# Hybrid attention block in fp32: the `p @ w_ple` tiles at the first norm, the second norm by halves of 256 tokens

## The chip, the cores and the metric

The kernel runs on one core of a Trainium2 chip. The metric is the device time of one execution in microseconds (us); lower is better. The kernel before was run three times.

## The reference

One transformer block over 512 tokens of width 1024, all in fp32. The output must be this, for one layer:

```python
h = rmsnorm(x, attn_pre_g)
proj = h @ w_in                      # split into the q, k, v of both attentions and gates
mix = concatenate([o_nsa, o_swa], -1) @ w_o
x = x + rmsnorm(mix, attn_post_g)    # the first norm of this text
h = rmsnorm(x, mlp_pre_g)
gu = h @ w_gate_up                   # 1024 x 5632
a, u = split(gu, [2816], -1)
a = causal_dwconv(a, conv_w, conv_b) # three taps along the tokens
y = (gelu(a) * u) @ w_down           # 2816 x 1024
x = x + rmsnorm(y, mlp_post_g)       # the second norm
e = p @ w_ple                        # 256 x 1024
x = x + e * sigmoid(x @ w_ple_gate)  # 1024 x 1024
```

`o_nsa` is an attention of eight heads over compressed, selected and windowed keys, `o_swa` one of eight heads over a window of 128 tokens with sinks. The change does not touch them.

## The kernel before

Activations lie transposed: channels on the 128 partitions, the 512 tokens along the free axis, so that a width of 1024 is eight tiles of 128x512. Every product of two fp32 matrices is made of three fp32r matmuls (`mm3`, line 130): the high part of the weight by the high part of the activation (L134), the low part of the weight by the high part (L137), the high part of the weight by the low part of the activation (L138). `weight` (L113) brings a weight tile in: SyncE issues its load into one of two raw buffers (`wr`, L127), ScalarE copies the high part out (L118), VectorE subtracts it for the low part (L122). The raw buffer is free for the next load when the subtraction is done.

The program is written phase by phase, and a scheduler that works on a simulated timeline sets the order of each engine's instructions; only where `keep_in_program_order` is called does the written order stand. On the chip each engine runs its list in that order and waits on semaphores.

- **Out-projection.** `out_proj` (L787) makes eight tiles. The first half of each, over the first four tiles of the attention's mix, is made earlier between attention work (`fill` in the names) and kept in `mo`. `out_proj` makes the second half by 12 matmuls (`mixmm`, L769 to L771) into one of two PSUM buffers `mm`, and VectorE adds it to `mo` (L802). ScalarE squares the sum (L219, L222), and GpSimd or, at the last tile, VectorE adds up the squares (L223). The last tile of the mix is written by ScalarE (L519) and GpSimd (L520) after VectorE's L517.
- **First norm.** `norm_add` (L811) wants the reciprocal root mean square of 512 tokens. `rstd_col` (L190) sums over partitions by small matmuls with ones (L194); VectorE (L198) and GpSimd (a power, L200) make the root. `rstd_row` (L203) brings it back to a row by four transposes (L207). Then, for each of eight tiles `c`, VectorE scales (L829) and adds to the residual (L830), ScalarE writes the high part of `h` (L834; L832 at the second norm), VectorE its low part one step later (L843; L841).
- **`p @ w_ple`.** Beside each norm stand four of the eight tiles of `p @ w_ple` (`ple_tile`, L859, six matmuls and a copy out of PSUM by ScalarE, L864): two before the column sums, one before the row, one after. Their operands are loaded and split by `ple_load` (L847), once for each half, at the last tile of the out-projection and of the down-projection.
- **Gate/up and down.** `chunkwise` (L884) makes the first four gate/up tiles together, chunk by chunk of the inner dimension, so that each `h` tile is used four times (12 matmuls) as it appears. Then `mlp_up` (L892) makes the others tile by tile, 24 matmuls each. `mlp_down` (L916) makes eight tiles of 66 matmuls.
- **Second norm and gate.** `norm_add` again, then `ple_gate` (L938): four tiles by `chunkwise`, four one by one, with sigmoid, product, sum and output.

All matmuls of these phases are 512 tokens wide. The pool of large tiles `u` has 23 slots, `wh` six (three weights).

## Time and profile before

| | |
|---|---|
| median of three runs | 686.6 us (685.11 to 687.87) |
| the profiled execution | 687.33 us |
| its span, first to last instruction | 685.4 us |
| mean granted TensorE clock | 0.992 |
| matmuls (PE) | 666.0 us busy, 97% |
| VectorE (DVE) | 400.1 us busy, 58% |
| ScalarE (ACT) | 325.2 us busy, 47% |
| GpSimd (POOL) | 170.8 us busy, 25% |
| DMA queue of the loads (q1) | 32.6% of 16 engines' span |

The profile comes from one execution. An instruction's row names its engine, its source line and its tiles, output first; `mlpup_pss` is a tile of the phase `mlpup` in the PSUM buffer `s`. The idle time of an engine before a row stands in brackets with what ended it. The row of a matmul is longer than the distance to the next one, since matmuls are pipelined. The clock is given as a share of its full rate: 1.00 is 2.4 GHz and 0.50 is 1.2 GHz.

### The profile page before, as it was taken

Reading aid. Unit: us, or ns where it says so; the run is one execution under the profiler, and the core shown is the slowest. Engines: PE = TensorE matmul, PEld = TensorE weight load, DVE = VectorE, ACT = ScalarE, POOL = GpSimd, SP = SyncE. Lnnn points to the kernel's source line nnn. Section 1 sums busy time; section 2 is a strip of 40 time slices with the busy share of each in tenths; the row PEclk is TensorE's granted clock in tenths of the full one; section 3 lists DMA queues with packets and bytes.
Section 4 is the critical chain, followed back from the end, with each engine's and each line's share of the span. In section 5 each row is a group of like instructions: output and inputs, shape, how many; then the busy total and the mean of one; then the engine's idle time right before and its main releaser. Section 6 shows DMA issues by size and latency. Waiting matters only on the chain.

```text
span 685.4 us, 8840 instructions
## 1 busy us (share of the span) xinstructions
PE 666.0 (97%) x3111; PEld 546.6 (80%) x3111; DVE 400.1 (58%) x808; ACT 325.2 (47%) x603; POOL 170.8 (25%) x235
## 2 busy tenths in 40 slices
PE   8999999999998998999999999999999999999996
PEld 7988767777786876888888888888888888887785
DVE  6785777877846569577555555455542232235853
ACT  7553778876867564354334333333432222233341
POOL 1112677755646244321111010111100000100000
PEclk9999999999998999999999999999999999999999
DMA  8547523101143252133322223332323323344032
GB/s 292 165 112 219 153 62 77 47 2 47 47 127 120 77 193 69 53 102 95 120 94 92 93 92 97 107 105 93 92 85 96 96 85 114 90 141 154 1 107 77
DMA packets 25115, 70.05 MB, mean 102 GB/s; under 512 B 3184, under 2 KB 4464, under 8 KB 25072
## 3 DMA queue, kind: packets, MB, share of 16 engines
q1 hardware_dynamic: 24928, 69.42, 32.6%
q8 instruction: 24, 0.39, 0.2%
q14 instruction: 19, 0.16, 0.1%
q10 hardware_dynamic: 144, 0.08, 0.0%
HBM read 60.05 MB, written 2.10 MB: 91 GB/s over the span
## 4 chain that ended last, share of the span: by engine, by line
PE 86%; DVE 5%; ACT 3%; DMA 2%; POOL 1%; issue 1%; SPq 0%; ACTq 0%; POOLq 0%; DVEq 0%
PE mlpup_pss L138 5%; PE mlpup_pss L137 5%; PE mlpup_pss L134 4%; PE mlpup_psmm L137 3%; PE mlpup_psmm L134 3%; PE mlpup_psmm L138 3%; PE nsa_pso L534 3%; PE mlpup_pst L138 3%; PE mlpup_pst L134 3%; PE mlpup_pst L137 3%; PE mlpdown_pss L134 2%; PE mlpdown_pss L138 2%; PE mlpdown_pss L137 2%; PE nsa_pst L501 2%; PE mlpdown_pst L138 1%; PE mlpdown_psmm L138 1%
## 5 line engine op out<-in xcount | busy, mean ns | idle before, releaser
L118 ACT ACTIVATE mlpup_wh<-mlpup_wr 128x1024 fp32r<-128x1024 f32 x40 | 42.3, 1061 | 84.5 <-PE mlpup_pss L137 28.9
L877 POOL TENSOR_TENSOR mlpup_s<-mlpup_s,r3b 128x512 f32<-128x512 f32 x22 | 29.2, 1331 | 188.0 <-ACT mlpup_s L876 188.0
L118 ACT ACTIVATE mlpdown_wh<-mlpdown_wr 128x1024 fp32r<-128x1024 f32 (+1 forms) x24 | 23.7, 989 | 84.7 <-PE mlpdown_pss L137 33.9
L122 DVE TENSOR_TENSOR mlpdown_wh<-mlpdown_wr,mlpdown_wh 128x1024 fp32r<-128x1024 f32 (+1 forms) x24 | 27.3, 1135 | 62.2 <-ACT mlpdown_wh L118 62.2
L122 DVE TENSOR_TENSOR mlpup_wh<-mlpup_wr,mlpup_wh 128x1024 fp32r<-128x1024 f32 x40 | 49.4, 1236 | 11.8 <-ACT mlpup_wh L118 11.7
L137 PE MATMUL mlpup_pss<-r_u,mlpup_wh 128*128 128x512 f32 x120 | 46.8, 390 | 0.2 <-DVE mlpup_wh L122 0.2
L134 PE MATMUL mlpup_pss<-r_u,mlpup_wh 128*128 128x512 f32 x120 | 46.8, 390 | 0.0
L138 PE MATMUL mlpup_pss<-r_u,mlpup_wh 128*128 128x512 f32 x120 | 46.7, 389 | 0.0
L523 POOL TENSOR_SCALAR nsa_u<-nsa_u,nsa_nrc,gate 128x512 f32<-128x512 f32 (+3 forms) x64 | 38.5, 617 | 22.2 <-DVE nsa_nrc L652 16.6
L621 ACT ACTIVATE nsa_u<-nsa_u,nsa_nnm 128x512 f32<-128x512 f32 (+3 forms) x64 | 35.4, 554 | 5.3 <-DVE nsa_nnm L617 5.1
L505 DVE TENSOR_TENSOR nsa_u<-nsa_pst,nsa_u 128x512 fp32r<-128x512 f32 (+1 forms) x43 | 29.0, 684 | 9.1 <-ACT nsa_u L503 8.8
L122 POOL TENSOR_TENSOR fill_wh<-fill_wr,fill_wh 128x512 fp32r<-128x512 f32 (+1 forms) x14 | 24.7, 1767 | 33.9 <-ACT fill_wh L118 33.9
L617 DVE CUSTOM_DVE_ANT_0 nsa_u<-nsa_pss,biastables_u 128x512 f32<-128x512 f32 (+3 forms) x64 | 29.9, 486 | 5.3 <-PE nsa_pss L555 4.9
L223 POOL TENSOR_TENSOR mlpdown_s<-mlpdown_s,mlpdown_s 128x512 f32<-128x512 f32 x6 | 7.8, 1295 | 100.2 <-ACT mlpdown_s L222 100.2
L876 ACT ACTIVATE mlpup_s<-mlpup_s 128x512 f32<-128x512 f32 x22 | 13.8, 631 | 38.6 <-DVE mlpup_s L875 38.6
L503 ACT ACTIVATE nsa_u<-nsa_pst 128x512 fp32r<-128x512 f32 (+1 forms) x43 | 25.1, 592 | 13.4 <-PE nsa_pst L501 13.1
L134 PE MATMUL mlpup_pst<-r_u,mlpup_wh 128*128 128x512 f32 x80 | 31.2, 390 | 0.0
L138 PE MATMUL mlpup_pst<-r_u,mlpup_wh 128*128 128x512 f32 x80 | 31.1, 389 | 0.0
L137 PE MATMUL mlpup_pst<-r_u,mlpup_wh 128*128 128x512 f32 x80 | 31.1, 389 | 0.0
L134 PE MATMUL mlpup_psmm<-r_u,mlpup_wh 128*128 128x512 f32 x80 | 31.1, 389 | 0.0
L137 PE MATMUL mlpup_psmm<-r_u,mlpup_wh 128*128 128x512 f32 x80 | 31.1, 389 | 0.0
L138 PE MATMUL mlpup_psmm<-r_u,mlpup_wh 128*128 128x512 f32 x80 | 31.1, 389 | 0.0
(386 smaller groups left out, 1937.9 us busy)
## 6 DMA issues: line engine op xcount, KB each, us to landing
mlpup_wr<-in_gu_dram SPq DMA_DIRECT2D x40, 512.0 KB, 3.3
mlpdown_wr<-in_down_dram SPq DMA_DIRECT2D x16, 512.0 KB, 3.5
fill_wr<-in_win_dram SPq DMA_DIRECT2D x6, 512.0 KB, 3.8
mlpdown_wr<-in_down_dram SPq DMA_DIRECT2D x8, 384.0 KB, 3.2
fill_u<-fill_u SPq DMA_DIRECT2D x20, 128.0 KB, 2.8
loadx_u<-in_xT_dram SPq DMA_DIRECT2D x8, 256.0 KB, 5.0
compress_u<-projk_u SPq DMA_DIRECT2D x16, 128.0 KB, 2.4
fill_wr<-in_wo_dram SPq DMA_DIRECT2D x8, 256.0 KB, 3.1
```

The source lines that it names most:

```text
L118: nc.scalar.activation(hi, raw, AF.Copy)
L122: eng.tensor_sub(lw, raw, hi.bitcast(F32))
L134: r = self.pin(mm(ps, hi, x[:, 0, :], start=start, stop=False))
L137: mm(ps, lo, x[:, 0, :], start=False, stop=False)
L138: mm(ps, hi, x[:, 1, :], start=False, stop=stop)
L503: nc.scalar.activation(t[:rows, 0, :], pt[:rows], AF.Copy)
L505: nc.vector.tensor_sub(lo, pt[:rows], t[:rows, 0, :].bitcast(F32))
L523: self.nc.gpsimd.tensor_scalar(ap, ap, col, gate, op0=ALU.mult, op1=ALU.mult)
L534: self.att(nc.tensor.matmul(po, v, rhs, start=start, stop=stop))
L617: nc.vector.tensor_tensor_reduce(dst, src, dist, op0=ALU.add, op1=ALU.min, scale=SLOPES[8 + 4 * g + r], scalar=3e38, accum_out=nm[:, r, b ...
L621: nc.scalar.activation(dst, dst, AF.Exp, bias=nm[:, r, b : b + 1], scale=-1.0, accum_out=sm[:, r, b : b + 1])
L877: nc.gpsimd.tensor_mul(c0, c0, self.r3)
```

## The change

Four things are done.

1. `ple_load` is called once, at the third tile of the out-projection, and loads both halves of `w_ple`; all eight `p @ w_ple` tiles stand at the first norm, four before the column sums, two before the row, two after. They alternate between the PSUM buffers `s` and `mm`.
2. The first four gate/up weights get buffers in `wh`, `tt` and `u`, and the two weights behind them are requested right after `chunkwise`.
3. The first three `w_ple_gate` weights are loaded and split during down tiles 2 to 4. The last down tile is made in two halves of 256 tokens. The norm of half 0 begins beside half 1, and the first four gate tiles are made half by half (`norm_half`, `gate_half`), with the sums and the transposes of half 1 in between. Two gate weights behind them are requested ahead.
4. `u` has 26 slots, and the program's scratch for software DMAs is set to 1024.

```diff
-SLOTS = {"u": 23, "kn": 4, "p": 6, "pt": 3, "tt": 2, "wh": 6}
+SLOTS = {"u": 26, "kn": 4, "p": 6, "pt": 3, "tt": 2, "wh": 6}
+H = T // 2
+HALF = [slice(h * H, (h + 1) * H) for h in range(2)]
...
     # out_proj, after the squares of tile c
+            if c == 2:
+                ple = self.ple_load()
+                self.phase = "outproj"
             if c == KC - 1:
-                ple = self.ple_load(0)
-                self.upw = [self.weight(io["gu"][i], tag="wh" if i < 3 else "u") for i in range(NB)]
+                self.upw = [self.weight(io["gu"][i], tag=("wh", "wh", "tt", "u")[i], keep=i > 1) for i in range(NB)]
...
     # norm_add
-        self.ple_tile(ple, 0)
-        self.ple_tile(ple, 1)
+        for i in range(4):
+            self.ple_tile(ple, i)
         y = self.rstd_col(acc, cname)
-        self.ple_tile(ple, 2)
+        for i in range(4, 6):
+            self.ple_tile(ple, i)
         r = self.rstd_row(y, cname, copy=False)
-        self.ple_tile(ple, 3)
-        self.e += ple[2]
+        for i in range(6, KC):
+            self.ple_tile(ple, i)
+        self.e = ple[2]
...
+    def norm_half(self, h, r, g, mo, x1, hs):
+        nc = self.nc
+        keep = self.tc.keep_in_program_order
+        ts = HALF[h]
+        for c in range(KC + 1):
+            if c < KC:
+                m = mo[c // 2][:, c % 2, ts]
+                x = x1[c // 2][:, c % 2, ts]
+                if h == 0:
+                    hs.append(self.u([P, 2, T], F32R))
+                keep(nc.vector.scalar_tensor_tensor(m, m, self.col(g + c), r[:, :H], op0=ALU.mult, op1=ALU.mult))
+                keep(nc.vector.tensor_add(x, x, m))
+                keep(nc.scalar.activation(hs[c][:, 0, ts], x, AF.Copy))
+            if c > 0:
+                x = x1[(c - 1) // 2][:, (c - 1) % 2, ts]
+                p = hs[c - 1]
+                keep(nc.vector.tensor_sub(p[:, 1, ts], x, p[:, 0, ts].bitcast(F32)))
+            yield
...
     # mlp_up, after chunkwise
+        ahead = [self.weight(io["gu"][NB + i], keep=True) for i in range(2)]
...
     # mlp_down: tiles 0 to 6 as before, and in the loop
+                if 2 <= c < 5:
+                    self.pgw.append(self.weight(io["wpg"][c - 2], tag=("u", "u", ("kn", "tt"))[c - 2]))
...
+        wts = [self.weight(io["down"][c][:, k.start * P : k.stop * P], len(k) * P) for k in ks]
+        raw = self.raw(io["wpg"][3])
...
+        last(0, range(NFF), ps0)
+        a0 = out(0, ps0)
+        last(1, range(5), ps1)
+        y = self.rstd_col(a0, "r4a")
+        last(1, range(5, 10), ps1)
+        r = self.rstd_row(y, "r4a", copy=False)
+        self.pgw.append(self.weight(raw, early=True, keep=True))
+        last(1, range(10, NFF), ps1)
+        first = self.norm_half(0, r, C_GMPOST, yo, self.x1, self.x2)
+        run(first, 4)
+        a1 = out(1, ps1)
+        self.pss = [self.ps(t) for t in ("s", "s", "s", "mm")]
+        run(first, 1)
+        self.gate_half(0, range(0, 3))
+        y = self.rstd_col(a1, "r4b")
+        run(first, 2)
+        self.gate_half(0, range(3, 5))
+        r = self.rstd_row(y, "r4b", copy=False, tag="o")
+        run(first, 2)
+        second = self.norm_half(1, r, C_GMPOST, yo, self.x1, self.x2)
+        run(second, KC + 1)
+        self.gate_half(0, range(5, KC))
+        self.gate_half(1, range(KC))
...
+    def gate_half(self, h, cs):
+        for k in cs:
+            for i in range(NB):
+                self.mm3(self.pss[i][:, HALF[h]], self.pgw[i], k * P, self.x2[k][:, :, HALF[h]], k == 0, k == KC - 1,
+                         keep=True)
```

In it `last(h, js, ps)` issues the matmuls of half `h` of the last down tile over the chunks `js`, and `out(h, ps)` copies the half out of PSUM, squares it and adds the squares.

The scheduler's order shows where the instructions went. VectorE at the start of the out-projection, before (L122 on `outproj_wh` splits an out-projection weight, L517 belongs to the last attention mix, L802 adds a finished tile):

```order
L122 TENSOR_TENSOR outproj_wh_2842<-outproj_wr_2839,outproj_wh_2841 128x512
L122 TENSOR_TENSOR outproj_wh_2865<-outproj_wr_2862,outproj_wh_2864 128x512
L517 TENSOR_TENSOR swa_s_2780<-swa_pso_2746,swa_s_2778 64x256 x2
L802 TENSOR_TENSOR fill_u_2285<-fill_u_2285,outproj_psmm_2824 128x512
L122 TENSOR_TENSOR outproj_wh_2888<-outproj_wr_2885,outproj_wh_2887 128x512
L802 TENSOR_TENSOR fill_u_2285<-fill_u_2285,outproj_psmm_2845 128x512
```

The same place in the change, where the lines are L125, L524 and L809, and L887 splits `p`:

```order
L125 TENSOR_TENSOR outproj_wh_2842<-outproj_wr_2839,outproj_wh_2841 128x512
L887 TENSOR_TENSOR pletiles_u_2887<-pletiles_u_2885,pletiles_u_2887 128x512
L887 TENSOR_TENSOR pletiles_u_2888<-pletiles_u_2885,pletiles_u_2888 128x512
L125 TENSOR_TENSOR outproj_wh_2865<-outproj_wr_2862,outproj_wh_2864 128x512
L524 TENSOR_TENSOR swa_s_2780<-swa_pso_2746,swa_s_2778 64x256 x2
L125 TENSOR_TENSOR pletiles_wh_2900<-pletiles_wr_2897,pletiles_wh_2899 128x1024
L125 TENSOR_TENSOR pletiles_wh_2906<-pletiles_wr_2903,pletiles_wh_2905 128x1024
L809 TENSOR_TENSOR fill_u_2285<-fill_u_2285,outproj_psmm_2824 128x512
L809 TENSOR_TENSOR fill_u_2285<-fill_u_2285,outproj_psmm_2845 128x512
```

Two splits of `p` came ahead of the third out-projection weight's, and both splits of `w_ple` ahead of the first sum.

ScalarE at the same place, before (L785 copies an early half tile out, L118 copies a weight's high part, L512 and L519 belong to the last attention mix):

```order
L785 ACTIVATE fill_u_2288<-fill_psmm_2762 128x512
L118 ACTIVATE outproj_wh_2864<-outproj_wr_2862 128x512
L785 ACTIVATE fill_u_2288<-fill_psmm_2795 128x512
L512 ACTIVATE swa_s_2778<-swa_pso_2746 64x512
L519 ACTIVATE swa_u_2441<-swa_s_2780 128x2x128
L118 ACTIVATE outproj_wh_2887<-outproj_wr_2885 128x512
```

And in the change (L792, L121, L519 and L526 are these lines there, L886 makes the high part of `p`):

```order
L792 ACTIVATE fill_u_2288<-fill_psmm_2762 128x512
L886 ACTIVATE pletiles_u_2887<-pletiles_u_2885 128x512
L886 ACTIVATE pletiles_u_2888<-pletiles_u_2885 128x512
L121 ACTIVATE outproj_wh_2864<-outproj_wr_2862 128x512
L792 ACTIVATE fill_u_2288<-fill_psmm_2795 128x512
L519 ACTIVATE swa_s_2778<-swa_pso_2746 64x512
L121 ACTIVATE pletiles_wh_2899<-pletiles_wr_2897 128x1024
L526 ACTIVATE swa_u_2441<-swa_s_2780 128x2x128
L121 ACTIVATE pletiles_wh_2905<-pletiles_wr_2903 128x1024
L121 ACTIVATE outproj_wh_2911<-outproj_wr_2909 128x512
```

The copies of `p` and of the two `w_ple` halves came in, the first half's ahead of the mix's last activation.

TensorE behind the first four gate/up tiles, before (L194 the column sums, then the first tile that is made alone):

```order
L138 MATMUL mlpup_psmm_3155<-r_u_3140,pletiles_wh_3036 128x512
L194 MATMUL mlpup_pst_3252<-ones,r_s_3086 128x1 x4
L134 MATMUL mlpup_pss_3327<-r_u_3087,mlpup_wh_3323 128x512
L137 MATMUL mlpup_pss_3327<-r_u_3087,mlpup_wh_3324 128x512
L138 MATMUL mlpup_pss_3327<-r_u_3087,mlpup_wh_3323 128x512
L134 MATMUL mlpup_pss_3327<-r_u_3092,mlpup_wh_3323 128x512
```

And in the change (L201, L140, L143 and L144 are these lines there; `mlpup_wh_3300` is the first of the weights in this piece, `mlpup_wh_3405` the third):

```order
L144 MATMUL mlpup_psmm_3195<-r_u_3180,outproj_wh_3044 128x512
L201 MATMUL mlpup_pst_3304<-ones,r_s_3126 128x1 x4
L140 MATMUL mlpup_pss_3367<-r_u_3127,mlpup_wh_3300 128x512
L140 MATMUL mlpup_pso_3409<-r_u_3127,mlpup_wh_3405 128x512
L143 MATMUL mlpup_pss_3367<-r_u_3127,mlpup_wh_3301 128x512
L144 MATMUL mlpup_pss_3367<-r_u_3127,mlpup_wh_3300 128x512
L140 MATMUL mlpup_pss_3367<-r_u_3132,mlpup_wh_3300 128x512
```

The second matmul behind the sums now belongs to another tile and takes a later weight.

## Rows read from the trace of the kernel before

**Rows 1.** The page, engines: busy us, share of the span, instructions
```profile
PE 666.0 (97%) x3111; PEld 546.6 (80%) x3111; DVE 400.1 (58%) x808; ACT 325.2 (47%) x603; POOL 170.8 (25%) x235
```

**Rows 2.** TensorE's waits, 229 to 300 us: total us, times, longest
```profile
PE mlpup_pss L134 <- ACT r_u L834: 1.4, 1, 1.4
...
PE mlpup_pss L138 <- DVE r_u L843: 0.6, 1, 0.6
```

**Rows 3.** Windows: engines' busy us, then granted clock, DMA share, GB/s
```profile
264.10:267.60 3.50, 3.50 (x10) 2.69 (x10) 3.43 (x5) 1.53 (x3) 2.86 (x2) 0.52 0.00 0
```

**Rows 4.** TensorE's timeline, first norm: start us, duration us, instruction, idle before
```profile
251.55 0.39 PE L134 MATMUL r_psmm<-pletiles_u,pletiles_wh 128*128 128x512 f32 x1
...
255.25 1.05 PE L194 MATMUL r_pst<-ones,outproj_s 128*128 128x1 f32 x8 [0.76 <-DVE outproj_s L223]
...
259.11 0.65 PE L207 MATMUL r_pst<-ident,r2c 128*128 128x128 f32 x4 [1.31 <-POOL r2c L200]
...
262.53 0.50 PE L134 MATMUL mlpup_pss<-r_u,pletiles_wh 128*128 128x512 f32 x1 [1.38 <-ACT r_u L834]
...
267.81 0.40 PE L134 MATMUL mlpup_pss<-r_u,pletiles_wh 128*128 128x512 f32 x1
```

**Rows 5.** Timeline of several engines, start of the out-projection
```profile
227.49 0.33 SPq L127 DMA_DIRECT2D outproj_wr<-in_wo_dram  x1
...
230.22 0.33 SPq L127 DMA_DIRECT2D outproj_wr<-in_wo_dram  x1
...
231.55 0.42 ACT L519 ACTIVATE swa_u<-swa_s 128x256 fp32r<-128x256 f32 x1 [0.98 <-DVE swa_s L517]
...
234.28 0.69 DVE L802 TENSOR_TENSOR fill_u<-fill_u,outproj_psmm 128x512 f32<-128x512 f32 x1 [2.76 <-PE outproj_psmm L771]
...
235.22 0.40 PE L769 MATMUL outproj_psmm<-nsa_u,outproj_wh 128*128 128x512 f32 x1
```

**Rows 6.** DMA issues, 218 to 250 us: count, KB, us from issue to landing
```profile
pletiles_wr<-in_gu_dram SPq DMA_DIRECT2D x2, 512.0 KB, 3.3
...
pletiles_wr<-in_wple_dram SPq DMA_DIRECT2D x1, 512.0 KB, 3.8
```

**Rows 7.** Timelines of VectorE and TensorE, end of the first four gate/up tiles
```profile
279.38 1.62 DVE L843 SCALAR_TENSOR_TENSOR r_u<-outproj_u,cols,r_u 128x512 fp32r<-128x512 f32 x2
...
287.67 0.48 PE L134 MATMUL mlpup_pss<-r_u,mlpup_wh 128*128 128x512 f32 x1
...
288.30 0.50 PE L137 MATMUL mlpup_pss<-r_u,mlpup_wh 128*128 128x512 f32 x1 [0.15 <-DVE mlpup_wh L122]
```

**Rows 8.** TensorE's timeline, second norm and the first four gate tiles
```profile
626.64 0.39 PE L134 MATMUL r_psmm<-pletiles_u,pletiles_wh 128*128 128x512 f32 x1
...
629.58 1.05 PE L194 MATMUL r_pst<-ones,mlpdown_s 128*128 128x1 f32 x8
...
631.98 0.65 PE L207 MATMUL r_pst<-ident,r4c 128*128 128x128 f32 x4
...
635.23 0.50 PE L134 MATMUL plegate_pss<-r_u,pletiles_wh 128*128 128x512 f32 x1 [1.21 <-ACT r_u L832]
...
639.94 0.39 PE L134 MATMUL plegate_pss<-r_u,pletiles_wh 128*128 128x512 f32 x1
...
657.62 0.39 PE L134 MATMUL plegate_pst<-r_u,plegate_wh 128*128 128x512 f32 x1
```

**Rows 9.** TensorE's timeline, six matmuls of 256 columns in the attention
```profile
176.23 0.28 PE L554 MATMUL swa_pss<-projq_u,fill_u 128*128 128x256 f32 x1
...
176.94 0.60 PE L501 MATMUL swa_pst<-ident,nsa_pc 128*32 128x128 f32 x4
```

**Rows 10.** Groups of weight loads by form: count, busy us, mean ns, idle
```profile
L555 PEld LDWEIGHTS swa_pss<-projq_u,fill_u 128*128 128x128 f32 x32 | 6.1, 190 | 0.3
```

**Rows 11.** The page, costliest groups: count, busy us, mean ns, idle before
```profile
L118 ACT ACTIVATE mlpup_wh<-mlpup_wr 128x1024 fp32r<-128x1024 f32 x40 | 42.3, 1061 | 84.5 <-PE mlpup_pss L137 28.9
...
L122 DVE TENSOR_TENSOR mlpdown_wh<-mlpdown_wr,mlpdown_wh 128x1024 fp32r<-128x1024 f32 (+1 forms) x24 | 27.3, 1135 | 62.2 <-ACT mlpdown_wh L118 62.2
```

More of the change, by code (lines that the diff above doesn't have):

```diff
@@ L908, in mlp_up @@
             for i in range(2):
-                wt = self.weight(io["gu"][2 * j + i])
+                wt = ahead.pop(0) if ahead else self.weight(io["gu"][2 * j + i])
                 ps = self.ps(ROT[n % 8])
@@ L920, in mlp_down @@
         yo = [self.u([P, 2, T]) for _ in range(4)]
+        ks = [range(0, 8), range(8, 16), range(16, NFF)]
+        self.pgw = []
         for c in range(KC):
[L922 to L931 removed]
@@ new lines, in mlp_down, with last, out @@
+        c = KC - 1
+        keep = self.tc.keep_in_program_order
+        wts = [self.weight(io["down"][c][:, k.start * P : k.stop * P], len(k) * P) for k in ks]
+        raw = self.raw(io["wpg"][3])
+        def last(h, js, ps):
+            for j in js:
+                self.mm3(ps, wts[j // 8], j % 8 * P, self.y[j][:, :, HALF[h]], j == 0, j == NFF - 1, keep=True)
+        def out(h, ps):
+            m = yo[c // 2][:, c % 2, HALF[h]]
+            sq = self.s([P, H])
+            keep(nc.scalar.activation(sq, ps, AF.Square))
+            keep(nc.vector.tensor_copy(m, ps))
+            a = acc[:, HALF[h]]
+            keep(nc.vector.tensor_add(a, a, sq))
+            return a
@@ new lines, in mlp_down @@
+        ps0, ps1 = (self.ps(t)[:, HALF[h]] for h, t in enumerate(("s", "mm")))
+        last(0, range(NFF), ps0)
[6 more added lines that the diff above has]
+        last(1, range(10, NFF), ps1)
+        self.phase = "norm"
+        self.x2 = []
+        run = lambda gen, n: [next(gen, None) for _ in range(n)]
```

79 lines of the change are left out of this document (40 added, 39 removed).

## The prediction

> **What bounds the kernel now.** I read the busy line of the page first. TensorE is busy 97% of the span, and the next engine 58% [rows 1]; so time can only come from TensorE's holes and from stretches at a lower clock, and extra work on ScalarE or VectorE costs nothing unless TensorE waits for it. Then I read TensorE's waits around the first norm. Four stand there: 1.4 us for the first `h` (ScalarE) and 0.6 for its low part (VectorE) [rows 2], and, as the timeline also shows ahead of the rows that waited, 1.31 for the reciprocal root that GpSimd computes and 0.76 for the sum of squares [rows 4]: 4.1 together. The windows come next: right behind these holes lies a stretch of 3.50 us with TensorE busy all of it and a granted clock of 0.52 [rows 3], which is the lower of its two levels (1.2 GHz), where it loses 3.5 x 0.48 = 1.7. Last comes TensorE's timeline around both norms, where the reader is to see the starts [rows 4, 8].
>
> The pitch of a full-width fp32r matmul is (657.62 - 639.94) / 78 = 0.2267 [rows 8], while a row of one shows 0.39 [rows 4]: a row's time holds some 0.16 that the next one overlaps. The column sums (1.05) and the row transposes (0.65) so take about 0.89 and 0.49 of the stream [rows 4].
>
> **(a) First norm.** From the first `p @ w_ple` matmul to the second gate/up chunk TensorE takes 267.81 - 251.55 = 16.26 [rows 4] for 24 + 12 matmuls. 36 x 0.2267 = 8.16, less 0.89 and 0.49 leaves 6.72 lost. The change has four tiles of six matmuls before the column sums in place of two, two between these and the transposes in place of one, and two behind. 12 more matmuls ahead cover 2.72; the column sums waited 0.76, so this goes. Between sums and transposes 12 matmuls again take 2.72; the same chain needed at most 631.98 - 629.58 = 2.40 at the second norm, where the transposes did not wait [rows 8]. The first norm's 3.86 [rows 4] was longer since a weight split stood on VectorE ahead of the small step. From transposes to first gate/up matmul 3.42 and 3.25 passed [rows 4, 8]; 0.49 + 12 x 0.2267 = 3.2 now cover it. What remains: 0.2 there, 0.5 for the low part of the first `h` (0.6 before [rows 2]), 0.2 for the second chunk's `h`, 0.3 for restarts, 1.2 in all. With no hole left above 0.6 I expect the clock to stay at its upper level. The gain is 6.72 - 1.2 = **5.5**. If the clock falls nevertheless it is 3.8, if nothing waits it is 6.1 (restarts and the low part remain): bounds 3.8 to 6.1. The 24 ple matmuls that come here leave the second norm, so they cancel.
>
> **(b) Start of the out-projection.** The loads and splits for `p @ w_ple` move from its last tiles to the third, and the order puts them into the middle of tiles 0 and 1, whose sums stand behind them. Before, the first sum is at 234.28 for 0.69, and tile 2, which takes its PSUM buffer, starts at 235.22 without waiting [rows 5]. Now the first `w_ple` half goes out where an out-projection weight went, at 227.49, and the second at about 230.22, when that raw buffer is split [rows 5]. A `w_ple` half lands after 3.8 [rows 6], so they come at 231.3 and 234.0. On ScalarE the copy of the first (1.06 [rows 11]) stands before the activation that writes the last attention mix: 231.3 + 1.06 = 232.36 against 231.55 [rows 5], some 0.8 later for the mix, and all of TensorE's tile 0 behind it. On VectorE both splits stand before the first sum: 234.0 + 1.06 + 1.14 [rows 11] = 236.2, with the sum 236.9, and tile 2 starts at 236.9 to 237.1 instead of 235.22. That covers the 0.8. The cost is **1.75**. Bounds: 0.8 if the second load comes early enough to hide (the mix alone), and 1.75 + 1.7 = 3.45 if a stretch at 1.2 GHz follows the hole as after the first norm. I take 1.75, which the rows give. The old places in the last tiles cost TensorE nothing (in time, the first of the four waits is that of the sums, behind them [rows 4]), so nothing comes back there but the earlier sum of squares of (a).
>
> **(c) Start of the gate/up loop.** Before, the third matmul behind the sums waits: 288.30 - 287.67 = 0.63, a hole of 0.40 [rows 7]. Now the second matmul takes the third later weight. Its load waits for the raw buffer of the first, which VectorE splits behind the norm's last low parts; these ended at 279.38 + 1.62 = 281.0 [rows 7], 18.5 after the first gate/up matmul at 262.53 [rows 4]. A copy that overlaps them in part and the split (1.06 and 1.14 [rows 11]) bring it to 20.3, the load (3.3 [rows 6]) and its copy to 24.7. TensorE at full clock is there after 96 x 0.2267, 0.7 of the stalls in (a), 0.89 and 0.23: 23.6. The hole is 1.1 in place of 0.40: **-0.7**. Bounds: 0 and -1.5 (no overlap, and a load of 3.8).
>
> **(d) Second norm.** From the end of the last down tile to the end of the first four gate tiles TensorE takes 657.62 - 626.64 = 30.98 [rows 8] for 24 + 96 matmuls: 120 x 0.2267 = 27.20, less 0.89 and 0.49 leaves 2.40 lost. By halves, all of it can hide: half 1 of the down tile is 66 matmuls of 256 columns, 7.8 us, over the chain of half 0 (2.40 + 3.25 at most [rows 8], and the copy out of PSUM); the chain of half 1 lies beside eight chunks of gate work, 12 matmuls each. There VectorE must make three half-width steps in each 1.42, and before it kept up with three full-width ones in each 2.72 with no wait behind the first chunk [rows 8]; a half-width step can take more than half of a full one, so the slack is thin, and the head start of half 0 is what it has. The price is the width. 256-wide matmuls ran at (176.94 - 176.23) / 6 = 0.118 [rows 9]. 66 + 66 + 96 + 96 = 324 of them replace 162 of 0.2267: 38.2 - 36.7 = 1.5 more. The second pair of sums and transposes costs 0.3 in restarts. The gain is 2.40 - 1.5 - 0.3 = **0.6**, bounds -1.8 (the 2.40 stays) and +2.1 (a pitch at half of 0.2267).
>
> Here a rule speaks against the change. The row first: in the six 256-wide matmuls each has its own weight load, whose rows last 0.190 [rows 10], and yet the pitch is 0.118 [rows 9], so the loads are hidden. The Trainium skill (TensorE: Matmul & The Clock Gate, Part 3, "The mechanism") says that a weight load overlaps matmuls in flight only where the row group differs, though it also names a background weight buffer. By that rule with full-height weights the loads would not hide and the width would double their number; six matmuls are a short run to refute it, so it is rival E.
>
> **At nothing.** The `w_ple_gate` weights split during down tiles 2 to 4: VectorE's splits there stood 62.2 us idle for their copies [rows 11]; without that cover each split would cost 1.14. The second load and split of `p` falls away from work that was hidden. The scratch size concerns no transfer that I found in the queues. The end (last gate tiles, output) is unchanged.
>
> **Sum.** 5.5 - 1.75 - 0.7 + 0.6 = 3.65 off. The profiled execution took 687.33, so it would be 683.7. That execution stands 0.7 above the median of the runs, 686.6; the forecast is **683.0**.
>
> **The rivals.** *A*, the sum: 683.0, own range 681.6 to 684.4, chance 0.50. *B*, the hole of (b) draws a half-clock stretch: its cost is 3.45, and the time 684.7. For it speaks that the first norm's holes were followed by one [rows 3]; against it, that 1.75 is shorter than these together. Chance 0.20. *C*, VectorE falls behind at the change of halves and the 2.40 of the second norm stays: (d) is -1.8, the time 685.4. The thin slack speaks for it, the head start of half 0 against. Chance 0.12. *D*, (b) costs its lower bound and (a) gives its upper one: 0.95 + 0.6 less, 681.4. Chance 0.12. *E*, slower: a long run of 256-wide matmuls is bound by weight loads. At the 0.190 of a load's row [rows 10] the 324 cost 324 x (0.190 - 0.118) = 23.3 more, and the time is 706.3. It decides from a pitch of 0.118 + 3.65 / 324 = 0.129 (no gain) and 0.140 (slower by 0.5%). Against it stand the rows at 0.118; for it, that these are six. Chance 0.06. That the change does not do what it says is out: the order shows all eight tiles at the first norm and the halves at the second.
>
> **Numbers.** About 0.5%, 3.4 us, is what a measurement of this kernel can tell from no change: 683.2. Faster by more: 0.32 of A's 0.50, D, and 0.04 of B, so 0.48; slower by more: E, 0.06; within: the rest, 0.46. The range 680.6 to 686.0 takes in A, B, C and most of D.
>
> **What would show it.** Right: TensorE's waits around the first norm below 1.5 together with the clock at full there; tile 2 of the out-projection 1.4 to 2.0 late behind VectorE's splits; a second matmul behind the first four gate/up tiles that waits about 1.1; 256-wide matmuls at 0.115 to 0.120; no wait above 0.5 at the second norm. Wrong: a clock of 0.5 anywhere new; 256-wide matmuls above 0.13; TensorE waiting for VectorE in the half gate tiles; or an out-projection that starts as before, by which (b) would be misread.

## The result, and the profile after

The changed kernel took 680.87 us (median of 7 runs, 680.56 to 682.72); the kernel before took 686.05 us beside it (7 runs, 684.52 to 687.87). The ratio is 0.9936, with a 95% interval of 0.9917 to 0.9954: 4.4 us less by the ratio, 5.2 by the medians. A second comparison gave 0.9957 (0.9942 to 0.9973), 3.0 less. The forecast was 683.0 against 686.6, which is 3.6 less and lies between the two.

The profiled execution took 680.73 us, its span 678.8, at a mean granted clock of 0.997. TensorE's busy line of the page, to be laid beside [rows 1]:

```profile
PE 662.9 (98%) x3273; PEld 552.1 (81%) x3273; DVE 403.9 (60%) x833; ACT 325.5 (48%) x610; POOL 171.7 (25%) x236
```

The matmuls rose from 3111 to 3273, since the halves are counted twice, and yet TensorE is busy 3.1 us less. So some of the 6.6 us between the two spans is clock and some is holes. TensorE's waits from 229 to 300 us, all that are left, answer to [rows 2]:

```profile
PE mlpup_pso L140 <- ACT mlpup_wh L121: 0.8, 1, 0.8
PE outproj_psmm L777 <- POOL swa_u L527: 0.6, 1, 0.6
PE outproj_psmm L776 <- DVE fill_u L809: 0.4, 1, 0.4
PE mlpup_pss L144 <- DVE r_u L854: 0.2, 1, 0.2
```

The four waits around the first norm are gone but for 0.2 us. Three new ones stand there: at the start of the gate/up loop (0.8) and at the start of the out-projection (0.6 and 0.4). The timeline of TensorE through the first norm answers to [rows 4]: first ple matmul, column sums, transposes, first gate/up matmul, second chunk.

```profile
250.88 0.40 PE L140 MATMUL r_pss<-pletiles_u,pletiles_wh 128*128 128x512 f32 x1
...
256.44 0.95 PE L201 MATMUL r_pst<-ones,outproj_s 128*128 128x1 f32 x8
...
260.13 0.60 PE L214 MATMUL r_pst<-ident,r2c 128*128 128x128 f32 x4
...
263.42 0.50 PE L140 MATMUL mlpup_pss<-r_u,outproj_wh 128*128 128x512 f32 x1
...
266.74 0.39 PE L140 MATMUL mlpup_pss<-r_u,outproj_wh 128*128 128x512 f32 x1
```

None of the five rows has idle time in front of it. From first to last it is 15.86 us, with twice the ple matmuls; without the 24 that came, 5.44, it is 10.42 where it was 16.26. The start of the out-projection answers to [rows 5]: VectorE's second split of `w_ple`, the first two sums behind it (one row), and tile 2.

```profile
232.55 1.23 DVE L125 TENSOR_TENSOR pletiles_wh<-pletiles_wr,pletiles_wh 128x1024 fp32r<-128x1024 f32 x1 [1.75 <-ACT pletiles_wh L121]
...
233.69 1.28 DVE L809 TENSOR_TENSOR fill_u<-fill_u,outproj_psmm 128x512 f32<-128x512 f32 x2
...
234.43 0.50 PE L776 MATMUL outproj_psmm<-nsa_u,outproj_wh 128*128 128x512 f32 x1 [0.43 <-DVE fill_u L809]
```

Behind the first four gate/up tiles, to [rows 7]: the load of the third later weight (its queue's row), its copy, and the matmul that waited for it.

```profile
283.87 0.33 SPq L133 DMA_DIRECT2D mlpup_wr<-in_gu_dram  x1
...
287.21 1.06 ACT L121 ACTIVATE mlpup_wh<-mlpup_wr 128x1024 fp32r<-128x1024 f32 x1 [1.96 <-PE mlpup_pst L201]
...
288.32 0.50 PE L140 MATMUL mlpup_pso<-r_u,mlpup_wh 128*128 128x512 f32 x1 [0.77 <-ACT mlpup_wh L121]
```

At the second norm, to [rows 8]: the first matmul of the last down tile, the first column sums 81 matmuls later, a first matmul of a gate chunk, and the end of the gate's halves 120 matmuls behind that.

```profile
611.29 0.28 PE L140 MATMUL mlpdown_pss<-mlpup_u,mlpdown_wh 128*128 128x256 f32 x1
...
621.00 0.50 PE L201 MATMUL mlpdown_pst<-ones,mlpdown_s 128*128 128x1 f32 x4
...
637.00 0.28 PE L140 MATMUL norm_pss<-norm_u,mlpdown_wh 128*128 128x256 f32 x1
...
651.27 0.39 PE L140 MATMUL plegate_pst<-norm_u,plegate_wh 128*128 128x512 f32 x1
```

TensorE's list of waits from 600 to 680 us is empty. The two pitches are (621.00 - 611.29) / 81 = 0.120 and (651.27 - 637.00) / 120 = 0.119.

**Where 6.6 us of span went.** The first out-projection matmul starts at 227.50, and at 229.71 before. That is 2.2 us ahead of everything that the change moves on TensorE: both programs issue the same 1155 matmuls up to there. The kernel before was profiled twice more (below) and reached the same matmul at 227.95 and 227.77. The table divides the time behind this point by differences of starts on TensorE's timeline; in the second and the last stage the ple matmuls in them are taken off at 0.2267 each, so that rows compare. The last column goes from the first out-projection matmul to the last matmul.

| profile | out-projection | first norm to second chunk, ple off | sums of the gate/up start to second matmul behind them | last down tile to end of first four gate tiles, ple off | all behind the point |
|---|---|---|---|---|---|
| before | 21.84 | 10.82 | 1.44 | 40.59 | 449.70 |
| before, second profile | 21.89 | 10.38 | 1.44 | 40.60 | 449.75 |
| before, third profile | 21.88 | 11.16 | 1.44 | 40.60 | 450.10 |
| changed | 23.38 | 4.98 | 2.06 | 39.98 | 445.33 |
| changed, second profile | 23.39 | 4.99 | 1.98 | 39.97 | 445.17 |

The change is worth 449.85 - 445.25 = 4.6 us behind the point (means), which the first ratio's 4.4 agrees with; 2 of the 6.6 belong to the executions that happened to be profiled. The second ratio's 3.0 is less: five of the six times of the changed kernel in it lie in the upper of two groups, which experiment 1 takes up.

### The profile page after: what moved, and what is told of

The parts are those of the page before. It is cut to its first block, busy times and chain, and to the rows that moved or that the text cites. A ratio compares the mean times of both kernels' runs of the same rounds, so it can differ in the third digit from the quotient of the medians.

```text
span 678.8 us, 9185 instructions
## 1 busy us (share of the span) xinstructions
PE 662.9 (98%) x3273; PEld 552.1 (81%) x3273; DVE 403.9 (60%) x833; ACT 325.5 (48%) x610; POOL 171.7 (25%) x236
## 4 chain that ended last, share of the span: by engine, by line
PE 90%; DVE 4%; ACT 2%; POOL 1%; DMA 1%; issue 1%; POOLq 0%; ACTq 0%; DVEq 0%
PE mlpup_pss L144 5%; PE mlpup_pss L143 4%; PE mlpup_pss L140 4%; PE mlpup_psmm L144 3%; PE mlpup_psmm L143 3%; PE mlpup_psmm L140 3%; PE nsa_pso L541 3%; PE mlpup_pst L144 3%; PE mlpup_pst L143 3%; PE mlpup_pst L140 3%; PE mlpdown_pss L140 3%; PE mlpdown_pss L143 3%; PE mlpdown_pss L144 3%; PE nsa_pst L508 2%; PE mlpdown_psmm L140 2%; PE mlpdown_psmm L143 2%
## 5 line engine op out<-in xcount | busy, mean ns | idle before, releaser
L121 ACT ACTIVATE mlpup_wh<-mlpup_wr 128x1024 fp32r<-128x1024 f32 x40 | 42.4, 1060 | 82.3 <-PE mlpup_pss L143 30.3
L125 DVE TENSOR_TENSOR mlpdown_wh<-mlpdown_wr,mlpdown_wh 128x1024 fp32r<-128x1024 f32 (+1 forms) x28 | 32.7, 1168 | 60.0 <-ACT mlpdown_wh L121 60.0
L121 ACT ACTIVATE mlpdown_wh<-mlpdown_wr 128x1024 fp32r<-128x1024 f32 (+1 forms) x28 | 28.0, 1000 | 84.0 <-PE mlpdown_pss L143 29.9
L125 DVE TENSOR_TENSOR mlpup_wh<-mlpup_wr,mlpup_wh 128x1024 fp32r<-128x1024 f32 x40 | 50.6, 1266 | 9.2 <-ACT mlpup_wh L121 9.1
L140 PE MATMUL mlpup_pss<-r_u,mlpup_wh 128*128 128x512 f32 x120 | 46.8, 390 | 0.0
L143 PE MATMUL mlpup_pss<-r_u,mlpup_wh 128*128 128x512 f32 x120 | 46.7, 389 | 0.0
L144 PE MATMUL mlpup_pss<-r_u,mlpup_wh 128*128 128x512 f32 x120 | 46.7, 389 | 0.0
L512 DVE TENSOR_TENSOR nsa_u<-nsa_pst,nsa_u 128x512 fp32r<-128x512 f32 (+1 forms) x43 | 29.0, 684 | 9.0 <-ACT nsa_u L510 8.7
L125 POOL TENSOR_TENSOR fill_wh<-fill_wr,fill_wh 128x512 fp32r<-128x512 f32 (+1 forms) x14 | 24.7, 1767 | 32.0 <-ACT fill_wh L121 32.0
L140 PE MATMUL mlpdown_pss<-mlpup_u,mlpdown_wh 128*128 128x512 f32 (+1 forms) x88 | 31.9, 363 | 0.0
L143 PE MATMUL mlpdown_pss<-mlpup_u,mlpdown_wh 128*128 128x512 f32 (+1 forms) x88 | 31.9, 363 | 0.0
L144 PE MATMUL mlpdown_pss<-mlpup_u,mlpdown_wh 128*128 128x512 f32 (+1 forms) x88 | 31.9, 363 | 0.0
L140 PE MATMUL mlpup_pst<-r_u,mlpup_wh 128*128 128x512 f32 x80 | 31.2, 390 | 0.0
L144 PE MATMUL mlpup_pst<-r_u,mlpup_wh 128*128 128x512 f32 x80 | 31.1, 389 | 0.0
L143 PE MATMUL mlpup_pst<-r_u,mlpup_wh 128*128 128x512 f32 x80 | 31.1, 389 | 0.0
```

The source lines that it names most:

```text
L121: h = nc.scalar.activation(hi, raw, AF.Copy)
L125: l = eng.tensor_sub(lw, raw, hi.bitcast(F32))
L140: r = self.pin(mm(ps, hi, x[:, 0, :], start=start, stop=False))
L143: mm(ps, lo, x[:, 0, :], start=False, stop=False)
L144: mm(ps, hi, x[:, 1, :], start=False, stop=stop)
L512: nc.vector.tensor_sub(lo, pt[:rows], t[:rows, 0, :].bitcast(F32))
```

## The experiments

The kernel before ran beside each; ratios are to it. What is said of a stage is read from the profile and holds to some 0.1 us, as the two profiles of the changed kernel do (the first norm of before alone differs by 0.8), and so tells more than the ratios.

**1. The changed kernel and the kernel before again.** No edit.

> The changed kernel once more, on the chip of the three below. Its first profile reaches the out-projection 2.21 us earlier than the one of before (first matmul at 227.50 against 229.71), because a stretch of 6.8 us at a granted clock of 0.51 is missing at 209 to 216 us, in work that the change does not touch. Theory 1 (chance of an execution): the stretch comes and goes from run to run in both kernels, so that the times of each kernel lie in two groups some 2 us apart (684.5 to 685.1 and 686.1 to 687.9 before; 680.6 to 680.9 and 682.2 to 682.7 after), and like compared with like the change is worth 3.9 to 4.4 us. Theory 2 (the change removes it): no profile of a kernel with the change shows the stretch, and the change is worth 6. The ratio to before says 0.994 by theory 1 and 0.991 by theory 2.

> The kernel before once more, for a second profile. Theory 1: the stretch at a granted clock of 0.51 at 209 to 216 us comes and goes, and so may the one at 264 to 267.5 behind the first norm: then the change is worth about 4.4 where before has the second stretch and 2.7 where it has not. Theory 2: the stretch behind the first norm is there in every execution of before, since the holes ahead of it are.

> The kernel before a third time, one look, for the same question: theory 1 says that at least one of the two half-clock stretches differs between the three profiles of before, theory 2 that the one behind the first norm is in all three with 3.4 us at half speed (16.2 us from the first ple matmul to the second gate/up chunk).

Measured: the changed kernel 0.9957 (0.9942 to 0.9973), six runs, one at 680.45 and five at 682.1 to 682.9. The kernel before beside itself gave 1.0015 (1.0004 to 1.0026) in the second profile's runs, so an interval of these is a little too narrow; the third profile comes from a single run, 685.83. The windows of the kernel before around its first norm, of the second profile and then of the third:

```profile
262.00:268.50 6.50, 5.86 (x23) 4.24 (x24) 6.43 (x8) 3.38 (x6) 3.29 (x2) 1.00 0.08 33
```

```profile
262.00:268.50 6.50, 6.21 (x20) 5.04 (x21) 6.40 (x9) 3.34 (x6) 3.32 (x3) 0.74 0.00 0
```

The stretch at half clock behind the first norm is in two of three profiles of before, as theory 1 of `before_b1` allows, with the same waits around it in all three (the second, whose clock stays at 1.00, even has 1.04 us more, in front of the second ple tile, and its stage is still the shortest). The first gate/up chunk takes 5.28 and 5.25 with the stretch and 3.69 without. In the profile of before shown first there is another one, in the attention:

```profile
209.40:216.20 6.80, 5.86 (x18) 4.57 (x19) 4.31 (x14) 5.59 (x22) 5.17 (x12) 0.51 0.39 111
```

It stands in that profile alone, of 13 that have the same attention. For the two groups of times some 2 us apart there is another candidate. This is TensorE's timeline near the start of the changed kernel, and of `ple_c5` below at the same instructions:

```profile
6.98 0.34 PE L348 MATMUL vnatural_pss<-loadx_u,loadx_u 128*128 128x408 f32 x1
...
7.16 0.35 PE L347 MATMUL vnatural_pss<-loadx_u,loadx_u 128*128 128x408 f32 x1
```

```profile
7.33 0.54 PE L347 MATMUL vnatural_pss<-loadx_u,loadx_u 128*128 128x408 f32 x1
...
7.67 0.54 PE L348 MATMUL vnatural_pss<-loadx_u,loadx_u 128*128 128x408 f32 x1
```

The pitch is 0.18 in the one and 0.34 in the other, until 10.7 us, at a granted clock of 1.00 in both, and the 1.9 us stay to the end. Five of the ten profiles of the changed kernel and its variants that are compared here reach the out-projection at 229.3 to 229.5 by this slow start, five at 227.5 to 227.7. The stretch in the attention is in none of them, but two profiles of before lack it as well. So theory 2 of `after_again` falls, and of its theory 1 the chance holds, not the cause: the stretch does not make the two groups of the changed kernel. Why the start is slow in some runs was not tried. None of the three profiles of before has it, though its times lie in two groups as well; whether the change makes it more frequent is open.

**2. The start of the out-projection (step b).** First, the loads later:

```diff
-            if c == 2:
+            if c == 5:
                 ple = self.ple_load()
```

> One number changed in the changed kernel: the loads and splits for p @ w_ple start at the sixth tile of the out-projection instead of the third, so that ScalarE and VectorE start the out-projection in the order of before. By the forecast's step (b) the hole at its start (0.60 and 0.43 us of waits in the changed kernel's profile, and a stage from its first matmul to the first ple matmul of 23.38 us against 21.84 before) goes: stage 21.8, time 1.5 lower than the changed kernel, 0.997 or 0.998 of it. Rival (the loads are only late elsewhere): the ple tiles or the sum of squares now wait at the end of the out-projection, the first norm's stage is 1 to 3 us longer and nothing is gained.

Measured: 0.9975 (0.9962 to 0.9989), and 447.70 us behind the point, 2.4 more than the changed kernel. The hole at the start is gone and a larger one stands further on. SyncE's queue (the second `w_ple` half, the next out-projection weight), and TensorE:

```profile
239.85 0.33 SPq L133 DMA_DIRECT2D pletiles_wr<-in_wple_dram  x1
...
243.97 0.33 SPq L133 DMA_DIRECT2D outproj_wr<-in_wo_dram  x1
...
247.73 0.50 PE L776 MATMUL outproj_psmm<-nsa_u,outproj_wh 128*128 128x512 f32 x1 [1.75 <-ACT outproj_wh L121]
```

The out-projection's weight could be requested only when a half of `w_ple` had left one of the two raw buffers, and TensorE waited 1.75 us. Behind that, its matmuls from 249.9 to 252.5 have a pitch of 0.43, at a granted clock of 0.50. The out-projection took 25.84. Neither theory had this: the wait moved, but into the loop and not to its end.

Then with raw buffers of their own (and with the edit of experiment 3):

```diff
-        return ph, [self.weight(io["wple"][j], tag=t) for j, t in enumerate(("pt", "u"))], e
+        raws = [self.raw(io["wple"][j], tag="p") for j in range(2)]
+        return ph, [self.weight(r, tag=t, early=True) for r, t in zip(raws, ("pt", "u"))], e
```

> The edit of the run w2_first, and the loads of p @ w_ple from the sixth tile on as in ple_c5, but the two halves of w_ple land in two free slots of the pool p instead of the two raw buffers that the out-projection's weights use. Theory (raw buffers): in ple_c5 an out-projection weight could be requested only at 243.97, when a half of w_ple was split, and TensorE waited 1.7 us for it; with own buffers nothing waits, the stage from the first out-projection matmul to the first ple matmul is 21.8 to 22.0 us (23.38 in the changed kernel, 25.84 in ple_c5), and the time is 2.2 to 2.5 lower than the changed kernel's, 678.3 or 680.2 by the two groups. Rival (engines): it is the copies and splits on ScalarE and VectorE ahead of the last attention mix that cost, wherever the data lie; the stage stays at 23 or more.

Measured: 0.9911 (0.9889 to 0.9933), 679.43 us, the lowest ratio of the study. But behind the point it takes 443.99, and the edit of experiment 3 alone 444.07, so what the raw buffers gave beyond that is 0.1. The out-projection took 23.04, so the theory held against `ple_c5` and not against the change. The rival had the rest. VectorE's second split, its step for the last attention mix, and TensorE:

```profile
228.40 1.22 DVE L125 TENSOR_TENSOR pletiles_wh<-pletiles_u,pletiles_wh 128x1024 fp32r<-128x1024 f32 x1
...
229.53 0.84 DVE L524 TENSOR_TENSOR swa_s<-swa_pso,swa_s 64x256 f32<-64x256 f32 x2
...
230.87 0.50 PE L776 MATMUL outproj_psmm<-swa_u,outproj_wh 128*128 128x512 f32 x1 [0.33 <-ACT swa_u L526]
```

The loads now came so early that the scheduler put both splits ahead of the mix. So one of them went to GpSimd:

```diff
-        return ph, [self.weight(r, tag=t, early=True) for r, t in zip(raws, ("pt", "u"))], e
+        return ph, [self.weight(r, tag=t, early=True, lo=o) for r, t, o in zip(raws, ("pt", "u"), ("pool", "dve"))], e
```

> As own_c5, but the low part of the first half of w_ple is made by GpSimd instead of VectorE, so that only one of the two splits (1.23 us) stands in VectorE's queue ahead of the last attention mix's step. Theory: in own_c5 that step began about 1.2 us late behind the two splits and TensorE's hole at the start of the out-projection (0.49 beyond a matmul's pitch, and 0.9 with the stretch behind it) came from there alone; with one split gone it starts in time, the stage from the first out-projection matmul to the first ple matmul is 21.9 to 22.1 us (23.04 in own_c5, 21.84 before), and the time is 1.0 lower than own_c5's 679.4, near 678.4. Rival: GpSimd's split (a 128x512 one took 1.29, so about 2.6) stands ahead of the same mix on GpSimd and the hole stays: 22.8 or more.

Measured: 0.9934 (0.9917 to 0.995), and the out-projection 23.92, 0.9 longer. GpSimd's split, VectorE's split of an out-projection weight beside it, and its step for the mix:

```profile
229.52 2.49 POOL L125 TENSOR_TENSOR pletiles_wh<-pletiles_u,pletiles_wh 128x1024 fp32r<-128x1024 f32 x1 [1.64 <-PE swa_pso L541]
...
229.68 2.88 DVE L125 TENSOR_TENSOR outproj_wh<-outproj_wr,outproj_wh 128x512 fp32r<-128x512 f32 x1
...
232.49 0.84 DVE L524 TENSOR_TENSOR swa_s<-swa_pso,swa_s 64x256 f32<-64x256 f32 x2
```

The rival's number was right (22.8 or more) and its place was wrong: it was not GpSimd's queue, but VectorE's subtraction that took 2.88 beside GpSimd's 2.49 instead of 0.69. It began 0.16 behind GpSimd's and ended 0.55 behind it.

**3. The start of the gate/up loop (step c).** The first later tile is written between sums and transposes, in program order, and the tile of the third weight is kept behind it:

```diff
-        _, self.r3 = self.rstd(self.acc3, "r3")
+        y = self.rstd_col(self.acc3, "r3")
+        ps2 = self.ps("s")
+        self.ordered = True
+        self.gemm(ps2, ahead[1], self.h2)
+        self.ordered = False
+        self.r3 = self.rstd_row(y, "r3")
```

> In the changed kernel, TensorE is made to finish the first later gate/up tile before it touches the third later weight. By the forecast's step (c) the 0.77 us wait (hole of 1.02) behind the first four gate/up tiles goes, since the weight that it now uses is split by 286.5 and TensorE arrives at 287.1: time 1.0 lower than the changed kernel. Rival (the third weight is late whatever comes first): the wait moves to the low part of the weight, as the 0.40 hole of before, or to the third weight's first matmul some 11 us later; nothing or 0.6 is gained.

Measured: 0.9931 (0.9914 to 0.9948), 679.85 us. The first two matmuls behind the sums:

```profile
288.81 0.48 PE L140 MATMUL mlpup_pss<-r_u,mlpup_wh 128*128 128x512 f32 x1
...
289.13 0.39 PE L143 MATMUL mlpup_pss<-r_u,mlpup_wh 128*128 128x512 f32 x1
```

Their distance is 0.32 instead of 1.25, nothing waits, and the stage is 1.13. Behind the point it takes 444.07, 1.2 less than the changed kernel, 0.9 of it in this stage. The theory holds.

Both one-place edits together (`c == 5` and this):

> The two edits together: by the theory they lie in different stages and add up, 2.5 lower than the changed kernel, 6.4 to 6.9 lower than before by the medians (ratio 0.990). Rival: one of the two stages takes back what the other gave, and the time is that of the better single edit.

Measured: 0.9952 (0.9937 to 0.9968). They don't add up, since the first does not gain: out-projection 23.74 with a wait of 1.3 for the same weight, and 0.6 more of wait for the root at the first norm.

**4. The place of the cover at the first norm (step a).** All ple tiles ahead of the sums:

```diff
-        for i in range(4):
+        for i in range(KC):
             self.ple_tile(ple, i)
         y = self.rstd_col(acc, cname)
-        for i in range(4, 6):
+        for i in range(KC, KC):
             self.ple_tile(ple, i)
         r = self.rstd_row(y, cname, copy=False)
-        for i in range(6, KC):
+        for i in range(KC, KC):
             self.ple_tile(ple, i)
```

> The changed kernel with all eight ple tiles ahead of the column sums of the first norm, none between sums and transposes and none behind: the same work, only its place differs. Theory (the place of the cover): the root's wait comes back with 1.5 us, the first h's with 2.8, so that the stage from the first ple matmul to the first gate/up matmul is 16.5 to 17 us in place of 12.54, and a stretch at a granted clock of about 0.5 follows for another 1.7; the time is 4 to 6 higher than the changed kernel's. Rival (the gain came from the splits that left VectorE's queue): the stage is within 0.7 of 12.54 and nothing follows.

Measured: 1.0001 (0.9986 to 1.0016). All of the gain is gone. TensorE's waits:

```profile
PE mlpup_pss L140 <- ACT r_u L845: 2.3, 1, 2.3
PE r_pst L214 <- POOL r2c L207: 1.4, 1, 1.4
```

From first ple to first gate/up matmul 16.45 us, then 5.09 for the first chunk in place of 3.32: the stretch at half clock is back (a granted clock of 0.54 from 268 to 272 us). The same work, in another place, takes 5.7 longer there. (Behind the sums of the gate/up start it has 1.13, as in experiment 3: its third weight had more time.)

Then the placing of before, with the other four tiles behind the gate/up sums:

```diff
-        for i in range(4):
+        for i in range(2):
             self.ple_tile(ple, i)
         y = self.rstd_col(acc, cname)
-        for i in range(4, 6):
-            self.ple_tile(ple, i)
+        self.ple_tile(ple, 2)
         r = self.rstd_row(y, cname, copy=False)
-        for i in range(6, KC):
-            self.ple_tile(ple, i)
+        self.ple_tile(ple, 3)
+        self.ple = ple
...
-    def ple_tile(self, ple, i):
+    def ple_tile(self, ple, i, tag=None):
...
-        _, self.r3 = self.rstd(self.acc3, "r3")
+        y = self.rstd_col(self.acc3, "r3")
+        for i in range(4, KC):
+            self.ple_tile(self.ple, i, "t")
+        self.r3 = self.rstd_row(y, "r3")
```

> The changed kernel with the placing of before at the first norm (two ple tiles ahead of the sums, one between, one behind); the other four stand behind the first four gate/up tiles and their column sums. Theory (cover): the first norm takes what it took before, 15.4 to 16.3 us from the first ple matmul to the second gate/up chunk, against 10.42 in the changed kernel when the 24 matmuls that left are taken off (15.86 less 5.44); the half-clock stretch comes back; behind the gate/up sums the wait for the third later weight goes (0.8). Time 4 to 5.5 higher than the changed kernel's. Rival (earlier splits): the first norm takes 12 or less, and the time is within 1.

> The kernel of ple_211 once more for its profile, since the execution that was profiled there ran at a lower clock throughout. Theory (cover): 15.4 to 16.3 us from the first ple matmul to the second gate/up chunk with a half-clock stretch, 13.8 to 14.6 without one; rival (earlier splits): 12 or less. Its time there was 0.9973 of before, 684.1, so 2 to 3 above the changed kernel and less than the 4 to 5.5 expected: either no half-clock stretch came, or less of the cover was lost than counted.

Measured: 0.9973 (0.9958 to 0.9988) and 0.9979 (0.9968 to 0.9991). The profiled execution of the first took 1700.81 us, with TensorE some 2.5 times as slow from end to end, so stages are read from the second. (The expectation of `ple_211_b` puts this down to a lower clock; the granted clock of that execution is 1.00.) There the first norm took 13.37 with 24 ple matmuls, 7.93 without them. Its waits:

```profile
PE mlpup_pss L140 <- ACT r_u L844: 1.3, 1, 1.3
PE r_pst L214 <- POOL r2c L207: 1.0, 1, 1.0
...
PE r_pst L201 <- DVE outproj_s L230: 0.2, 1, 0.2
```

The waits for the root and the first `h` are those of before, to 0.3 us. The wait for the sum of squares is 0.2 in place of 0.76, the one for the low part of the first `h` 0.2 in place of 0.6, and no stretch at half clock came. So both theories had a part: 7.93 - 4.98 = 2.95 of the gain is cover. The other 2.4 to 3.2 (10.38 to 11.16 less 7.93) is the stretch, where before has it, and, judging by the waits that shrank, what left VectorE's queue at the end of the out-projection. No run takes these two apart.

**5. Without the halves (step d).** Last down tile, norm and gate tiles at 512 tokens:

```diff
-        last(0, range(NFF), ps0)
-        a0 = out(0, ps0)
...
-        self.gate_half(0, range(5, KC))
-        self.gate_half(1, range(KC))
+        for j in range(NFF):
+            self.mm3(ps, wts[j // 8], j % 8 * P, self.y[j], j == 0, j == NFF - 1, keep=True)
...
+        y = self.rstd_col(acc, "r4")
+        r = self.rstd_row(y, "r4", copy=False)
...
+        for k in range(KC):
+            for i in range(NB):
+                self.mm3(self.pss[i], self.pgw[i], k * P, self.x2[k], k == 0, k == KC - 1, keep=True)
```

> The changed kernel with its last down tile, second norm and first four gate tiles at the full 512 tokens, all ple tiles left at the first norm. Theory (the halves pay for the ple tiles that left): without cover TensorE waits for the square and sum, then 1.5 us for the root (2.40 less the sums' 0.89), 2.8 for the first h (3.25 less 0.49) and about 0.5 for its low part, and the clock may fall behind that for another 1.7. From the first matmul of the last down tile to the end of the first four gate tiles it takes 44 to 46.5 us in place of 39.98; the time is 4 to 6.5 higher than the changed kernel's. Rival (the width costs as much as it hides): full width saves 1.5 and the waits are short, the time is within 1 of the changed kernel's.

Measured: 1.0058 (1.0038 to 1.0078), slower than before. The stage takes 48.08. Its waits, and two windows behind them:

```profile
PE norm_pss L140 <- ACT norm_u L1008: 2.2, 1, 2.2
PE mlpdown_pst L201 <- DVE mlpdown_s L994: 2.1, 1, 2.1
PE mlpdown_pst L214 <- POOL r4c L207: 1.4, 1, 1.4
```

```profile
633.00:637.00 4.00, 1.77 (x6) 0.97 (x5) 3.02 (x5) 0.83 (x2) 0.00 (x0) 0.50 0.25 99
637.00:642.00 5.00, 4.89 (x12) 3.61 (x12) 4.93 (x8) 1.70 (x3) 0.00 (x0) 0.50 0.00 0
```

The waits are 5.7 together, and the clock stands at its lower level, 1.2 GHz, through both windows. The theory holds, and its price was too low (8.1 us against 4 to 6.5): the halves are worth 8.1 us where the ple tiles are gone, the 9 us at half clock included.

## Why the prediction was right

The measured 680.87 lies in the stated range by its lower end (680.6), and below the sum's own range (681.6 to 684.4). The steps came out as forecast, two of them in part by luck, as (a) and (b) tell. Rival D's time (681.4) came nearest, but not by its way: the out-projection cost far more than its lower bound of 0.8.

**(a) First norm.** Forecast 5.5, measured 5.4 to 6.2 (10.38 to 11.16 less 4.98). All four waits went as it said; 0.19 remains in front of the low part where 0.5 was put, and 0.28 at the second chunk. The clock stayed up. The reasons share the gain otherwise than the step had it: the cover of the moved tiles is worth 2.95 (`ple_211_b`), and the rest, by subtraction, came with the splits that no longer stand in VectorE's queue before the sums and the transposes, and with the stretch at half clock, which is not in every execution of before. The step took that stretch as certain. In the profile without it, 1.04 of another wait make up for most of it; without either the gain would have been 10.38 - 1.04 - 4.98 = 4.4 (an estimate from these rows), so that the 5.5 was met in part by luck. The step's upper bound of 6.1 is also a slip: restarts and low part, 0.3 and 0.5, leave 5.9.

**(b) Start of the out-projection.** Forecast a cost of 1.75, measured 1.54. In its larger part the mechanism is the forecast's: second half of `w_ple` split at 232.55 behind its load, both sums behind that, tile 2 late by 1.42 against the first matmul; the loads landed after 3.2 and 3.3 instead of 3.8. The late mix is luck. It came 0.8 late as forecast, but ScalarE's activation was only 0.1 later. The rest is GpSimd's step, before and after, which took twice as long beside VectorE's split of the first half (229.57 to 230.80):

```profile
232.05 0.74 POOL L520 TENSOR_TENSOR swa_u<-swa_s,swa_u 128x256 fp32r<-128x256 f32 x1 [3.98 <-ACT swa_u L519]
```

```profile
229.92 1.46 POOL L527 TENSOR_TENSOR swa_u<-swa_s,swa_u 128x256 fp32r<-128x256 f32 x1 [4.07 <-ACT swa_u L526]
```

It ended at 231.38, and TensorE's wait of 0.60 is for it. Rival B's stretch at half clock did not follow here (a granted clock of 1.00); behind the longer wait in `ple_c5` one did.

**(c) Start of the gate/up loop.** Forecast 0.7, measured 2.06 - 1.44 = 0.62, with a hole of 1.02 where 1.1 was put. The chain is row by row as told: load at 283.87, copy at 287.21, matmul at 288.32.

**(d) Second norm.** Forecast 0.6, measured 0.62. There was no wait at all, so rival C fell. VectorE's three half-width steps come every 1.18 us at the second half, where TensorE's chunk takes 1.42, and its first low part there ended 1.16 before TensorE used it (638.93 against 640.09). The slack was thinnest earlier, where the sums of half 1 stand between: the low part of the fifth chunk of half 0 on VectorE, and the matmul that uses it, 0.23 after its end.

```profile
633.52 0.42 DVE L875 TENSOR_TENSOR norm_u<-outproj_u,norm_u 128x256 fp32r<-128x256 f32 x1
...
634.17 0.28 PE L144 MATMUL norm_pss<-norm_u,mlpdown_wh 128*128 128x256 f32 x1
```

The pitch, 0.119 to 0.120, is that of the six matmuls of [rows 9] and one per cent over, and rival E's threshold of 0.129 is not reached. The loads are hidden: the 256 columns between a half-width and a full matmul cost 0.2267 - 0.119 = 0.108, which leaves 0.011 of the pitch for all else, a new weight included (an estimate from the two pitches). The Trainium skill (TensorE: Matmul & The Clock Gate, Part 3, "The mechanism") says that a weight load overlaps matmuls in flight only with another row group, and beside it names a background weight buffer. The first alone does not hold in this trace, where every one of these weights is a full 128x128: in the window of 620 to 636 us the loads' row is busy all of the time, and so is the matmuls':

```profile
620.00:636.00 16.00, 16.00 (x137) 16.00 (x136) 11.50 (x30) 4.26 (x9) 1.41 (x2) 1.00 0.11 34
```

**Sum.** Forecast 3.65 from the steps, measured 4.6 behind the point by the profiles, of which (a) to (d) hold 5.8 - 1.54 - 0.58 + 0.62 = 4.3 and the last gate tiles 0.2, whose weights are requested ahead (the step had them unchanged). The forecast came out at 683.0 where 680.9 was measured: of these 2.1, 5.2 - 3.6 = 1.6 is more gain by the medians than forecast, and 0.5 is that the kernel before also had a lower median here (686.05). Of the 1.6, 4.6 - 3.65 = 0.95 is shown in the stages; that the rest comes from more runs with the quick start fits the two groups of times, and is only argued. The second comparison, with fewer such runs, gave less than the forecast.

## What to carry to other kernels

A reduction in front of a long chain of matmuls needs independent matmuls placed at each of its waits: the same eight tiles made 5.7 us of difference by where they stood, a stretch at half clock included. If such filler is taken from one place, something must replace it, and half-width tiles of the work on both sides did so here, and were worth 8.1 us (again with a stretch at half clock) with their own price taken off. A load that is moved earlier goes through the raw buffers, the queue and the splitting engine of what already stands there, so all three have to be looked at before the place is chosen.

## What the runs showed of the hardware

- VectorE's subtraction of two 128x512 tiles took 2.88 us beside a GpSimd subtraction of 2.49 that had begun 0.16 earlier, and 0.69 without (`split_c5`). The other way round, GpSimd's step took 1.46 instead of 0.74 where VectorE's split had begun 0.35 earlier (the changed kernel). In both pairs the later one ended 0.55 to 0.58 behind the earlier, as if it had waited the other out. The Trainium skill (GPSIMD Engine Reference, 1. Specifications) says that GpSimd shares its SBUF interfaces with VectorE and that VectorE's instructions with two SBUF inputs contend; these traces agree.
- The first matmuls ran at a pitch of 0.34 instead of 0.18 until about 10.7 us in five of ten profiles of the changed kernel and its variants, worth 1.9 us for the whole run, at a granted clock of 1.00; none of the three profiles of before has it.
- The stretch at half clock behind the first norm of before came in two of three profiles, and not in the one with the most waits ahead of it; behind the 1.75 us wait in `ple_c5` the clock was at 0.50 from 249.9 to 252.5, and with the 5.7 us of waits in `no_halves` for all of 9 us.
- 256-wide fp32r matmuls with a new 128x128 weight each ran for 120 in a row at 0.119, 5% over half of a 512-wide one's 0.2267.
- In the 1700.81 us execution of `ple_211` the 256-wide matmuls near 1600 us had a pitch of some 0.3 instead of 0.12, though the granted clock stands at 1.00 and VectorE's busy time (404.1) is that of the changed kernel (403.9). What slowed TensorE alone stays open; the record of the clock does not show it. One execution of `both_fixed`, which was not profiled, took 1338.16 us, its granted clock on record 1.00 as well.
